# Shift and scale of the modulation summed along rows on VectorE, in a two-block transformer kernel on one core

## The chip, the core and the metric

The kernel runs on one core of a Trainium2 chip. The core has five engines that run side by side and wait for each other through semaphores: TensorE (matmuls, PE in the profile), VectorE (DVE), ScalarE (ACT), GpSimd (POOL) and SyncE (SP), which here issues most transfers. The metric is the device time of one execution in microseconds (us).

## What is computed

A batch of one sequence of 256 positions and 1024 features goes through two blocks. What the change touches is the adaptive modulation of the first block: a vector `c` of 1024 values is turned into nine rows of 1024, a shift, a scale and a gate for each of three sublayers.

```python
mods = (silu(c) @ w_ada + b_ada).reshape(1, 9, 1024)     # w_ada: 1024 x 9216, f32
shift = lambda i: mods[:, 3 * i]
scale = lambda i: mods[:, 3 * i + 1]
gate = lambda i: mods[:, 3 * i + 2][:, None, :]

n = rmsnorm(h, g_pre[0]) * (1 + scale(0)) + shift(0)      # sublayer 0: feed-forward
f = (silu(n @ w_gate) * (n @ w_up)) @ w_down
h = h + 0.5 * gate(0) * rmsnorm(f, g_post[0])
# sublayer 1: two attentions side by side ("mixer"); sublayer 2: a second feed-forward
# second block: two attention layers and two MLPs, no modulation
```

## The kernel before

All weights, 1024-column blocks of 128 partitions (512 KB each), come in one stream in the order of a list that `plan()` makes; `pump_one` issues transfers up to seven items ahead and works off one item. A weight item is split in two parts for precision: ScalarE casts it (`wh`, line 489) and VectorE takes the remainder (`wl`, line 495). Each product is then three matmuls: high by high, high by low, low by high. `nh` and `nl` are the same two parts of the normalised, modulated activations, with the features in the partitions and 256 positions along the row.

A modulation item is not used as a weight. `ada_item` handles it by VectorE: with the rows of `w_ada` in the partitions, a 128x1024 block is multiplied by one value of `silu(c)` per partition and added to a running tile `ada` (line 460; for the first block of a row a plain multiplication, line 458). After eight blocks (`k` from 0 to 7) `ada` holds partial sums that still have to be summed over the 128 partitions. For the shifts and scales of sublayers 1 and 2 (rows 3, 4, 6, 7) `ada_columns` does that by eight one-column matmuls with a vector of ones, which give the row as columns, features in the partitions: `ac_b` holds the shifts, `ac_a` the scales times the gain. For the gates (rows 2, 5, 8) `ada_gate` sums by matmuls with a matrix of ones. The gates' bias enters at the first block, through a tile `bz` that is zero but for its first row.

The shift and scale of sublayer 0 come in another cut, `ad0`, because the opening needs them piece by piece: an item `("ad0", k, q)` holds, for 128 features of the shift and 128 of the scale, four of the eight row blocks. ScalarE does the first of eight 128x256 multiplications (line 448), VectorE adds the other seven (line 450), and `reduce_` sums the tile over the partitions by two one-column matmuls.

`start_ffn` is the opening, written out by hand. `h[0]` and `h[1]`, the two halves of the positions, are squared and summed (line 607), scaled (`y`), transposed by TensorE (line 632) and kept as `yT`. Then the first seven column groups of the feed-forward (`M0`) are computed row block by row block: for each `k` from 0 to 7 `coefficients(k)` makes 128 features of `ac_b` and `ac_a`, applies them (`y2`, line 1023) and casts (line 1024), `low` makes `nl`, and `first(k, 0)` and `first(k, 1)` run 21 matmuls each against the items `s0` (gate and up weights, 448 KB each). I call one `k` a step. Each engine works its instructions in the order in which the code issues them.

Of the kernel before, what the change touches and what calls it, by code (L numbers as in the profile page):

```python
# [10 lines left out]
F32 = mybir.dt.float32  # L11
# [50 lines left out]
M0 = 7  # L62
# [45 lines left out]
def plan():  # L108
# [23 lines left out]
    for k in range(2):  # L132
        out += [(("ad0", k, 0), 1024), (("ad0", k, 1), 1024)]
        if k == 0:
            out.append((("s0", 0, 0), M0 * P))
    for k in range(8):
        out.append((("s0", k, 1), M0 * P))
        if k < 6:
            out += [(("ad0", k + 2, 0), 1024), (("ad0", k + 2, 1), 1024)]
        if k < 7:  # L140
            out.append((("s0", k + 1, 0), M0 * P))
# [54 lines left out]
def pack_stream(a):  # L196
# [11 lines left out]
    def piece(key):  # L208
        n = key[0]
        if n == "ad0":  # L210
            _, k, q = key
            w = a["w_ada"][0][512 * q:512 * q + 512]
            w = np.concatenate([w[:, P * k:P * k + P], w[:, D + P * k:D + P * k + P]], axis=1)
        elif n == "s0":
# [107 lines left out]
def model_kernel(ctx, tc, x, stream, cols, const, rows, bada, relb, onehot, out):  # L322
# [71 lines left out]
    for i in range(2):  # L394
        nc.sync.dma_start(h[1][:, 512 * i:512 * i + 512], x[tk(1), 512 * i:512 * i + 512])
# [16 lines left out]
    bz = cp.tile([P, D], F32, name="bz")  # L412
    pool.memset(bz, 0.0)
    nc.sync.dma_start(bz[0:1, :], bada[2:3, :])
# [15 lines left out]
    ada_end = {}  # L430
    bg = []

    def load(key, n, off):
        raw = w1k("raw0") if key[0] == "ad0" else rawp.tile([P, RAWC], F32, tag="raw", name="raw")
# [3 lines left out]
    def ada_item(key, raw):  # L438
        if key[0] == "ad0":
            _, k, q = key  # L440
            if q == 0:
                ada_acc["a"] = w256("ada")
            a = ada_acc["a"]
            for j in range(4):
                c = sc[:, 4 * q + j:4 * q + j + 1]
                r = raw[:, j * 2 * P:(j + 1) * 2 * P]
                if q == 0 and j == 0:
                    act.activation(a, r, AF.Copy, scale=c)
                else:
                    dve.scalar_tensor_tensor(a, r, c, a, op0=ALU.mult, op1=ALU.add)  # L450
            return
        _, j, k = key
        if k == 0:
            ada_acc[j] = w1k("ada")
        a = ada_acc[j]
        c = sc[:, k:k + 1]
        if k == 0 and j % 3 < 2:
            dve.tensor_scalar(a, raw, c, None, op0=ALU.mult)
        else:
            dve.scalar_tensor_tensor(a, raw, c, a if k else bz, op0=ALU.mult, op1=ALU.add)  # L460
        if k == 1 and j in (2, 5):
            nc.sync.dma_start(bz[0:1, :], bada[j + 3:j + 4, :])
        if k == 7:
            bg.append(ada_end[j](j, a))
            if j == 4:
                st["lo"] = "dve"
# [3 lines left out]
    def pump_one():  # L470
# [7 lines left out]
        if key[0] in ("ada", "ad0"):  # L478
# [25 lines left out]
    def pump(ahead=None):  # L504
        ahead = st["ahead"] if ahead is None else ahead
        while st["i"] < len(items):
            if items[st["i"]][0][0] not in ("ada", "ad0") and st["w"] >= st["rel"] + ahead + extra():
# [356 lines left out]
    bp1 = cp.tile([P, 72], F32, name="bp1")  # L864
    G = {}

    def ada_columns(j, a):
        for _ in range(4 if j == 3 else 2):
            yield
        ps = bank()  # L870
        for k in range(8):
            mm(ps[:, 2 * k:2 * k + 1], a[:, k * P:(k + 1) * P], ones[:, 0:1], start=(k == 0))
        v = ps.rearrange("p (k two) -> p k two", two=2)[:, 0:8, 0]
        i, sh = j // 3, j % 3 == 0
        if sh:
            dve.tensor_tensor(ac_b[:, i, :], v, cl[:, C_BADA + 8 * j:C_BADA + 8 * j + 8], op=ALU.add)
        else:
# [1093 lines left out]
```

## Time and profile before

| | |
|---|---|
| median of 3 runs | 1164.33 us (1160.9, 1164.33, 1165.6) |
| profiled execution | 1167.6 us |
| its span, first to last instruction | 1165.8 us |
| TensorE busy | 1120.3 us, 96% of the span |
| VectorE busy | 746.2 us, 64% |
| ScalarE busy | 603.4 us, 52% |
| transfers | 230.27 MB, mean 198 GB/s |

The shares are averages over stretches with different limits. What ends last in a stretch is read from the chain of work (what released each instruction, followed back from the end), from the timeline, and from the wait printed at a row's end in brackets with the instruction that ended it. The last part of the time, from 1165.8 to 1167.6 us, lies outside the span.

### The profile page before, as it was taken

Reading aid. Unit: us, or ns where it says so; the run is one execution under the profiler, and the core shown is the slowest. Engines: PE = TensorE matmul, PEld = TensorE weight load, DVE = VectorE, ACT = ScalarE, POOL = GpSimd, SP = SyncE. Lnnn points to the kernel's source line nnn. Section 1 sums busy time; section 2 is a strip of 40 time slices with the busy share of each in tenths; the row PEclk is TensorE's granted clock in tenths of the full one; section 3 lists DMA queues with packets and bytes.
Section 4 is the critical chain, followed back from the end, with each engine's and each line's share of the span. In section 5 each row is a group of like instructions: output and inputs, shape, how many; then the busy total and the mean of one; then the engine's idle time right before and its main releaser. Section 6 shows DMA issues by size and latency. Waiting matters only on the chain.

```text
span 1165.8 us, 18854 instructions
## 1 busy us (share of the span) xinstructions
PE 1120.3 (96%) x7268; PEld 1012.5 (87%) x7268; DVE 746.2 (64%) x1286; ACT 603.4 (52%) x1159; POOL 144.4 (12%) x152
## 2 busy tenths in 40 slices
PE   5999999899999899999999799999999999999997
PEld 5998999799888799999887678999998888999996
DVE  5987866689667776455656657555566746655554
ACT  5564444554576544343564566444457655544443
POOL 1001000204000300000058630000003200000001
PEclk9999999999999999999999999999999999999999
DMA  8978977468447385545544234655544523755540
GB/s 289 352 265 318 374 291 244 139 217 325 162 148 250 142 308 190 205 168 184 178 158 149 89 124 143 210 193 188 191 152 140 199 92 126 251 182 184 194 148 37
DMA packets 65920, 230.27 MB, mean 198 GB/s; under 512 B 7275, under 2 KB 8691, under 8 KB 65702
## 3 DMA queue, kind: packets, MB, share of 16 engines
q1 hardware_dynamic: 63798, 225.07, 55.8%
q10 hardware_dynamic: 1776, 3.29, 0.8%
q8 instruction: 57, 0.93, 0.3%
q0 software_dynamic: 256, 0.71, 0.2%
q14 instruction: 33, 0.27, 0.1%
HBM read 227.98 MB, written 2.63 MB: 198 GB/s over the span
## 4 chain that ended last, share of the span: by engine, by line
PE 76%; DVE 10%; ACT 7%; issue 3%; POOL 3%; DMA 0%; SPq 0%; POOLq 0%; ACTq 0%; DVEq 0%
PE mm L547 39%; PE acc L547 35%; DVE wl L495 2%; ACT wh L489 2%; POOL wl L495 2%; PE mm L632 1%; DVE ada L450 1%; DVE ada L460 1%; ACT junk L607 1%; ACT s L1491 1%; POOL sm L604 1%; ACT s L1346 1%; DVE s L1569 0%; DMA h<-in_x_dram 0%; DVE y L701 0%
## 5 line engine op out<-in xcount | busy, mean ns | idle before, releaser
L495 DVE TENSOR_TENSOR wl<-raw,wh 128x1024 fp32r<-128x1024 f32 (+4 forms) x318 | 380.4, 1210 | 86.5 <-ACT wh L489 86.4
L489 ACT ACTIVATE wh<-raw 128x1024 fp32r<-128x1024 f32 (+3 forms) x350 | 354.7, 1034 | 14.0 <-DMA raw<-in_stream_dram 12.9
L547 PE MATMUL mm<-nl,wh 128*128 128x256 f32 x1128 | 314.6, 284 | 0.0
L547 PE MATMUL mm<-nh,wh 128*128 128x256 f32 x1128 | 314.4, 284 | 0.0
L547 PE MATMUL mm<-nh,wl 128*128 128x256 f32 x1128 | 314.3, 283 | 0.0
L547 PEld LDWEIGHTS mm<-nl,wh 128*128 128x128 f32 x1128 | 214.5, 192 | 3.0
L547 PEld LDWEIGHTS mm<-nh,wh 128*128 128x128 f32 x1128 | 214.5, 192 | 3.0
L547 PEld LDWEIGHTS mm<-nh,wl 128*128 128x128 f32 x1128 | 214.2, 192 | 0.0
L547 PE MATMUL acc<-wl,fh 128*128 128x512 f32 x372 | 120.4, 390 | 1.5 <-DVE wl L495 1.5
L547 PE MATMUL acc<-wh,fh 128*128 128x512 f32 x372 | 120.9, 392 | 0.0
L547 PE MATMUL acc<-wh,fl 128*128 128x512 f32 x372 | 119.7, 389 | 0.0
L1089 ACT ACTIVATE rl<-mm 128x256 f32<-128x256 f32 x64 | 24.6, 384 | 160.9 <-PE mm L547 160.9
L495 POOL TENSOR_TENSOR wl<-raw,wh 128x512 fp32r<-128x512 f32 (+2 forms) x64 | 81.7, 1305 | 203.1 <-ACT wh L489 203.1
L604 POOL TENSOR_TENSOR sm<-sm,nhalf 128x1 f32<-128x1 f32 (+1 forms) x36 | 21.5, 597 | 631.4 <-DVE sm L613 566.9
L1090 DVE TENSOR_TENSOR ff<-rl 128x256 f32<-128x256 f32 x64 | 27.2, 425 | 102.5 <-ACT rl L1089 102.5
L914 ACT ACTIVATE sg<-mm 128x256 f32<-128x256 f32 x38 | 14.4, 382 | 137.8 <-PE mm L547 137.8
L547 PEld LDWEIGHTS acc<-wl,fh 128*128 128x128 f32 x372 | 69.9, 188 | 18.1 <-DVE wl L495 3.2
L547 PEld LDWEIGHTS acc<-wh,fl 128*128 128x128 f32 x372 | 69.9, 188 | 14.8
L547 PE MATMUL acc<-wh,nh 128*128 128x512 f32 (+3 forms) x208 | 79.2, 404 | 1.1 <-ACT nh L637 1.1
L547 PE MATMUL acc<-wh,nl 128*128 128x512 f32 (+3 forms) x208 | 75.3, 386 | 0.6 <-DVE nl L638 0.6
L547 PE MATMUL acc<-wl,nh 128*128 128x512 f32 (+3 forms) x208 | 75.1, 385 | 0.0
L547 PEld LDWEIGHTS acc<-wh,fh 128*128 128x128 f32 x372 | 65.5, 189 | 9.1
(322 smaller groups left out, 1638.3 us busy)
## 6 DMA issues: line engine op xcount, KB each, us to landing
raw<-in_stream_dram SPq DMA_DIRECT2D x395, 512.0 KB, 4.6
raw<-in_stream_dram SPq DMA_DIRECT2D x16, 448.0 KB, 6.5
raw<-in_stream_dram SPq DMA_DIRECT2D x8, 384.0 KB, 3.4
raw<-in_stream_dram SPq DMA_DIRECT2D x8, 292.0 KB, 3.2
gp<-in_rows_dram SPq DMA_DIRECT2D x3, 512.0 KB, 6.6
wide<-scr ACTq DMA_DIRECT2D x1, 1536.0 KB, 9.3
raw<-in_stream_dram SPq DMA_DIRECT2D x4, 320.0 KB, 3.0
h<-in_x_dram SPq DMA_DIRECT2D x4, 256.0 KB, 3.6
```

Source lines behind the costliest of these rows:

```text
L450: dve.scalar_tensor_tensor(a, r, c, a, op0=ALU.mult, op1=ALU.add)
L460: dve.scalar_tensor_tensor(a, raw, c, a if k else bz, op0=ALU.mult, op1=ALU.add)
L489: act.activation(wh[:, 0:n], raw, AF.Copy)
L495: e.tensor_tensor(wl[:, u:v], raw[:, u:v], wh[:, u:v].bitcast(F32), op=ALU.subtract)
L547: pe.matmul(o, l, r, start=start, stop=True, skip_group_check=True)
L604: pool.tensor_tensor(o, v, nhalf[:, 0:v.shape[-1]], op=ALU.pow)
L607: act.activation(junk(p_.shape[-1]), p_, AF.Square, scale=1.0 / math.sqrt(n) if scale is None else scale, accum_out=acc_)
L632: pe.transpose(tp[:, j * P:(j + 1) * P], src[:, j * P:(j + 1) * P], ident)
L914: act.activation(sg, ps[:, 0:S], AF.Silu)
L1089: act.activation(rl, ps[:, 0:S], AF.Relu)
L1090: dve.tensor_tensor(ff, rl, rl, op=ALU.mult)
L1346: act.activation(s[:, c], s[:, c], AF.Exp, bias=nm[:, t:t + 1], accum_out=rsum[:, 2 * t + j:2 * t + j + 1])
```

## The change

Shift and scale rows are packed transposed: 128 features in the partitions, all 1024 inputs along the row. One VectorE instruction multiplies such a block with `cb`, a tile that holds `silu(c)` in every partition, and sums along the row; the sum starts at the bias and lands in one column of `ac_b` (for a scale, times the gain, in `ac_a`). The sum over partitions on TensorE, `ada_columns`, `reduce_` and the cut `ad0` go. `cb` is made in the opening by eight TensorE matmuls, whose one side is a column of `c` read 128 times, and a silu on ScalarE. The gates keep their way, but their bias now starts the sum: eight ScalarE copies of 128x128 (the identity times a bias column) fill `ada` before the first block.

The opening is written in another order. The first modulation block is fetched ahead of `h[1]`, five more items behind it. The squares of `h[1]` are summed by VectorE with the same new operation. The transposes go by pairs of features' blocks into one bank each, the first step's activations are made straight from there, in both parts (`nh` and `y2`) by ScalarE from the same source, and the first group of matmuls runs high by high, high by low of the weights, then the low activations.

```diff
-        out += [(("ad0", k, 0), 1024), (("ad0", k, 1), 1024)]
+        out += [(("ada", 0, k), 1024), (("ada", 1, k), 1024)]
...
-            w = a["w_ada"][0][P * k:P * k + P, 1024 * j:1024 * j + 1024]
+            if j % 3 == 2:
+                w = a["w_ada"][0][P * k:P * k + P, 1024 * j:1024 * j + 1024]
+            else:
+                w = a["w_ada"][0][:, 1024 * j + P * k:1024 * j + P * k + P].T
...
+        i = j // 3
+        if j % 3 < 2:
+
+            dst, init, scale = (ac_b, cl[:, C_BADA + 8 * j + k:C_BADA + 8 * j + k + 1], 1.0) if j % 3 == 0 else \
+                (ac_a, bpg[:, 8 * i + k:8 * i + k + 1], cl[:, C_GPRE + 8 * i + k:C_GPRE + 8 * i + k + 1])
+            dve.tensor_tensor_reduce(out=raw, in0=raw, in1=cb, scale=scale, scalar=init, op0=ALU.mult, op1=ALU.add,
+                                     accum_out=dst[:, i, k:k + 1])
         else:
-            dve.scalar_tensor_tensor(a, raw, c, a if k else bz, op0=ALU.mult, op1=ALU.add)
...
+            if k == 0:
+                ada_acc[j] = w1k("ada")
+                for m in range(8):
+                    act.activation(ada_acc[j][:, m * P:(m + 1) * P], ident, AF.Copy,
+                                   scale=cl[:, C_BADA + 8 * j + m:C_BADA + 8 * j + m + 1])
+            a = ada_acc[j]
+            dve.scalar_tensor_tensor(a, raw, sc[:, k:k + 1], a, op0=ALU.mult, op1=ALU.add)
...
+        cps = [bank() for _ in range(2)]
+        for k in range(8):
+            mm(cps[k // 4][:, k % 4 * P:k % 4 * P + P], cl[:, C_C + k:C_C + k + 1].broadcast_to([P, P]), ident,
+               start=(k % 4 == 0))
+        raws.append(load(*items[0]))
+        for i in range(2):
+            nc.sync.dma_start(h[1][:, 512 * i:512 * i + 512], x[tk(1), 512 * i:512 * i + 512])
...
+        for i in range(2):
+            act.activation(cb[:, 512 * i:512 * i + 512], cps[i], AF.Silu)
+        r0 = inv_rms(ss[0])
...
+            dve.tensor_tensor_reduce(out=ys[1][hf], in0=half(1, hf), in1=half(1, hf), scale=1.0 / D, scalar=0.0,
+                                     op0=ALU.mult, op1=ALU.add, accum_out=ss[1][:, hf:hf + 1])
...
         def coefficients(k):
-            ps = red[0]
-            dve.tensor_tensor(ac_b[:, 0, k:k + 1], ps[:, 0:1], cl[:, C_BADA + k:C_BADA + k + 1], op=ALU.add)
...
+            src = yT[:, k, :] if k else tps[0][:, 0:S]
+            a, b = ac_a[:, 0, k:k + 1], ac_b[:, 0, k:k + 1]
+            act.activation(n[0][:, k, :], src, AF.Identity, scale=a, bias=b)
             y2 = w256("y2")
-            act.activation(y2, yT[:, k, :], AF.Identity, scale=ac_a[:, 0, k:k + 1], bias=ac_b[:, 0, k:k + 1])
-            act.activation(n[0][:, k, :], y2, AF.Copy)
+            act.activation(y2, src, AF.Identity, scale=a, bias=b)
```

VectorE in a step of the opening, before: partial sums with the two coefficient instructions between them, then `nl` of the next step and the remainders of two weight items.

```order
L450 SCALAR_TENSOR_TENSOR ada<-raw_225,sc,ada 128x256 x3
L1019 TENSOR_TENSOR ac_b<-mm,cl 128x1
L1020 SCALAR_TENSOR_TENSOR ac_a<-mm,bp_115,cl 128x1
L450 SCALAR_TENSOR_TENSOR ada<-raw_231,sc,ada 128x256 x4
L1028 TENSOR_TENSOR nl<-y_346,nh 128x256
L495 TENSOR_TENSOR wl<-raw,wh 128x896 x2
```

After, in the same step (`ISA` is the new operation and, below it, the read of its accumulator):

```order
L439 ISA raw_217,ac_b<-raw_217,cb,cl 128x1024
L439 ISA ac_b 128x1
L439 ISA raw_220,ac_a<-raw_220,cb,bpg,cl 128x1024
L439 ISA ac_a 128x1
L996 TENSOR_TENSOR nl<-y_315,nh 128x256
L481 TENSOR_TENSOR wl<-raw,wh 128x896 x2
```

Seven partial sums and two coefficient instructions have become two reductions with a read each; the coefficients of a step are made two steps ahead, and no TensorE work stands between them and ScalarE.

TensorE at the start of the program, before: the transposes of `y`, the sum of the first partial sums over the partitions, the first matmuls.

```order
L632 MATMUL mm<-kc,y 128x128 x16
L547 MATMUL mm<-onesr,ada 128x1 x2
L547 MATMUL acc<-nh,wh 128x256 x4
L547 MATMUL mm<-nh,wh 128x256 x3
L547 MATMUL acc<-nl,wh 128x256 x4
L547 MATMUL mm<-nl,wh 128x256 x3
```

After (`mm<-kc,cl` are the copies of `c` into all partitions):

```order
L533 MATMUL mm<-kc,cl 128x128 x8
L984 MATMUL mm<-kc,y 128x128 x16
L533 MATMUL acc<-nh,wh 128x256 x4
L533 MATMUL acc<-nh,wl 128x256 x4
L533 MATMUL acc<-nl,wh 128x256 x4
L533 MATMUL mm<-nh,wh 128x256 x3
```

The two matmuls on `ada` that stood ahead of the first step's matmuls are gone, eight on `cl` now stand ahead of the transposes, and in the first group the weights' low part comes ahead of the activations' low part.

ScalarE where the opening ends and the remainder of the feed-forward begins, before: the casts of two weights, then the silu of the seven column groups (`sg`), their cast (`Fh`) and the next weights.

```order
L489 ACTIVATE wh<-raw 128x1024 x2
L420 DMA kc<-in_const_dram 128x512
L914 ACTIVATE sg<-mm 128x256 x2
L918 ACTIVATE Fh<-sg 128x256
L489 ACTIVATE wh<-raw 128x1024
L914 ACTIVATE sg<-mm 128x256
L918 ACTIVATE Fh<-sg 128x256
```

After:

```order
L475 ACTIVATE wh<-raw 128x1024 x2
L415 DMA kc<-in_const_dram 128x512
L880 ACTIVATE sg<-mm 128x256
L445 ACTIVATE ada<-kc,cl 128x128 x8
L880 ACTIVATE sg<-mm 128x256
L884 ACTIVATE Fh<-sg 128x256
L475 ACTIVATE wh<-raw 128x1024
L880 ACTIVATE sg<-mm 128x256
```

Eight copies that start the first gate's sum now stand between the first two `sg`, ahead of the next weights' casts.

## Rows read from the trace of the kernel before

**Rows 1.** The page's part 4: the chain that ended last, shares by engine.

```profile
PE 76%; DVE 10%; ACT 7%; issue 3%; POOL 3%; DMA 0%; SPq 0%; POOLq 0%; ACTq 0%; DVEq 0%
```

**Rows 2.** Timeline, opening: start us, us, engine, line, operation, out<-in, count [idle before]

```profile
7.87 0.63 ACT L607 ACTIVATE junk<-h 128x512 bf16<-128x512 f32 x1 [1.04 <-DMA h<-in_x_dram]
...
8.92 0.56 POOL L604 TENSOR_TENSOR sm<-sm,nhalf 128x1 f32<-128x1 f32 x1 [1.90 <-DVE sm L613]
...
9.51 1.33 ACT L993 ACTIVATE y<-h,sm 128x512 f32<-128x512 f32 x2 [0.92 <-POOL sm L604]
...
16.50 0.60 ACT L1023 ACTIVATE y<-yT,ac_b,ac_a 128x256 f32<-128x256 f32 x1 [3.32 <-DVE ac_a L1020]
...
17.45 0.93 ACT L489 ACTIVATE wh<-raw 128x896 fp32r<-128x896 f32 x1
...
18.44 1.23 PE L547 MATMUL acc<-nh,wh 128*128 128x256 f32 x4 [2.36 <-ACT wh L489]
...
28.10 0.64 PE L547 MATMUL acc<-nh,wh 128*128 128x256 f32 x4
```

**Rows 3.** Windows: stretch, length, busy by engine, TensorE's granted clock, DMA share, GB/s

```profile
2.00:15.00 13.00, 3.94 (x16) 3.14 (x16) 4.98 (x12) 7.23 (x17) 3.18 (x6) 1.00 0.95 346
18.00:28.00 10.00, 9.56 (x46) 9.47 (x47) 9.20 (x21) 4.30 (x8) 0.00 (x0) 1.00 0.78 273
30.00:57.00 27.00, 26.44 (x216) 25.68 (x214) 26.11 (x57) 14.07 (x23) 0.00 (x0) 1.00 0.97 358
```

**Rows 4.** Timeline of one step of the opening, VectorE and TensorE

```profile
33.79 2.09 DVE L495 TENSOR_TENSOR wl<-raw,wh 128x896 fp32r<-128x896 f32 x2
...
35.80 1.52 DVE L450 SCALAR_TENSOR_TENSOR ada<-raw,sc,ada 128x256 f32<-128x256 f32 x3
...
36.18 0.50 PE L547 MATMUL mm<-onesr,ada 128*128 128x1 f32 x4
...
36.55 0.72 PE L547 MATMUL acc<-nh,wh 128*128 128x256 f32 x4
...
39.38 0.42 DVE L1028 TENSOR_TENSOR nl<-y,nh 128x256 fp32r<-128x256 f32 x1
...
39.49 0.74 PE L547 MATMUL acc<-nh,wh 128*128 128x256 f32 x4 [0.19 <-ACT wh L489]
...
39.71 2.08 DVE L495 TENSOR_TENSOR wl<-raw,wh 128x896 fp32r<-128x896 f32 x2
```

**Rows 5.** Chain of work in order of time: start us, us, what

```profile
67.68 11.88 PE mm L547 x99
```

**Rows 6.** VectorE's groups by form (busy us, mean ns); last row: tile ljk, min/median/max ns

```profile
L460 DVE SCALAR_TENSOR_TENSOR ada<-raw,sc,ada 128x1024 f32<-128x1024 f32 x49 | 62.8, 1283 | 0.0
...
L1488 DVE CUSTOM_DVE_ANT_0 s<-mm,cmaskw 128x256 f32<-128x256 f32 x24 | 10.1, 420 | 21.2 <-PE mm L547 21.2
...
L1488 DVE CUSTOM_DVE_ANT_0 s<-mm,cmaskw 128x128 f32<-128x128 f32 x24 | 6.8, 285 | 0.0
...
L1488 DVE DVE_READ_ACCUMULATOR2_ANT sm<- 128x1 f32 x48 | 3.9, 82 | 0.0
...
L1500 DVE CUSTOM_DVE_ANT_0 ljk<-lamin x2: 217/221/225, 573.9 to 574.2; 128x64 f32<-128x64 f32 x2
```

**Rows 7.** Timeline of TensorE, the first row of shifts behind the opening

```profile
159.83 1.84 PE L547 MATMUL mm<-onesr,ada 128*128 128x1 f32 x16
```

**Rows 8.** Chain of work in order of time, first mixer and its end

```profile
273.28 0.66 DVE ada L458
...
276.30 1.19 DVE ada L460
...
362.87 1.68 PE mm L547 x16
```

**Rows 9.** Timeline: VectorE behind the opening, ScalarE in the first mixer

```profile
70.46 1.22 DVE L495 TENSOR_TENSOR wl<-raw,wh 128x1024 fp32r<-128x1024 f32 x1
...
365.08 2.18 ACT L644 ACTIVATE db<-mm,cl 128x128 fp32r<-128x128 f32 x8 [2.50 <-PE mm L632]
```

More of the change, by code (lines that the diff above doesn't have):

```diff
@@ L138, in plan @@
         if k < 6:
[L139 removed]
+            out += [(("ada", 0, k + 2), 1024), (("ada", 1, k + 2), 1024)]
         if k < 7:
@@ L321, in model_kernel @@
 @with_exitstack
-def model_kernel(ctx, tc, x, stream, cols, const, rows, bada, relb, onehot, out):
+def model_kernel(ctx, tc, x, stream, cols, const, rows, relb, onehot, out):
     nc = tc.nc
@@ L438, in ada_item @@
     def ada_item(key, raw):
[L439 to L451, printed above, removed]
-        _, j, k = key
[L453 to L458, printed above, removed]
-        else:
-            dve.scalar_tensor_tensor(a, raw, c, a if k else bz, op0=ALU.mult, op1=ALU.add)
[L461 to L466, printed above, removed]
+        _, j, k = key
+        i = j // 3
[4 more added lines that the diff above has]
+                                     accum_out=dst[:, i, k:k + 1])
+        else:
+            if k == 0:
[5 more added lines that the diff above has]
+            dve.scalar_tensor_tensor(a, raw, sc[:, k:k + 1], a, op0=ALU.mult, op1=ALU.add)
+            if k == 7:
+                bg.append(ada_gate(j, a))
+        if k == 7 and j == 4:
+            st["lo"] = "dve"
     raws = []
@@ L506, in pump @@
         while st["i"] < len(items):
-            if items[st["i"]][0][0] not in ("ada", "ad0") and st["w"] >= st["rel"] + ahead + extra():
+            if items[st["i"]][0][0] != "ada" and st["w"] >= st["rel"] + ahead + extra():
                 if not spare or ahead < NR:
@@ L863, in model_kernel @@
     ac_b = cp.tile([P, 3, 8], F32, name="ac_b")
-    bp1 = cp.tile([P, 72], F32, name="bp1")
+    bpg = cp.tile([P, 24], F32, name="bpg")
     G = {}
[L867 to L877, printed above, removed]
-            tmp = small(8)
-            dve.tensor_tensor(tmp, v, bp1[:, 8 * j:8 * j + 8], op=ALU.add)
-            dve.tensor_tensor(ac_a[:, i, :], tmp, cl[:, C_GPRE + 8 * i:C_GPRE + 8 * i + 8], op=ALU.mult)
     def ada_gate(j, a):
@@ L981, in start_ffn @@
         yT = big(F32, "yT")
-        dve.tensor_scalar(bp1, cl[:, C_BADA:C_BADA + 72], 1.0, None, op0=ALU.add)
-        ss = [small(2) for _ in range(2)]
-        for t in range(2):
-            for hf in range(2):
-                square_sum(half(t, hf), D, ss[t][:, hf:hf + 1])
-        tps = []
-        for t in range(2):
-            r = inv_rms(ss[t])
-            ys = [w512("y") for _ in range(2)]
-            for hf in range(2):
-                if t:
-                    act.activation(ys[hf], half(t, hf), AF.Copy, scale=r)
-                else:
-                    dve.tensor_scalar(ys[hf], half(t, hf), r, None, op0=ALU.mult)
-            tps += [transposes(ys[hf], 4) for hf in range(2)]
+        dve.scalar_tensor_tensor(bpg.rearrange("p (a b) -> p a b", b=8),
+                                 cl[:, C_BADA:C_BADA + 72].rearrange("p (a b) -> p a b", b=24)[:, :, 8:16], 1.0,
+                                 cl[:, C_GPRE:C_GPRE + 24].rearrange("p (a b) -> p a b", b=8), op0=ALU.add, op1=ALU.mult)
@@ L997, in start_ffn @@
+        r1 = inv_rms(ss[1])
+        for hf in range(2):
+            act.activation(ys[1][hf], half(1, hf), AF.Copy, scale=r1)
         pump_one()
         pump_one()
-        for i, tp in enumerate(tps):
-            act.activation(yT[:, 4 * (i % 2):4 * (i % 2) + 4, tk(i // 2)], tp.rearrange("p (a b) -> p a b", a=4), AF.Copy)
-        acc = [abank() for _ in range(4)] + [bank() for _ in range(M0 - 4)]
-        sums = [ada_acc["a"]]
-        red = [None]
-        def ada_half():
-            pump_one()
-            if sums[-1] is not ada_acc["a"]:
-                sums.append(ada_acc["a"])
```

71 lines of the change are left out of this document (36 added, 35 removed).

## The prediction

> **What bounds the kernel now.** I read the chain of work that ended last first: TensorE holds 76% of it, VectorE 10%, ScalarE 7% [rows 1]. So the kernel is a TensorE kernel with a few stretches where something else ends last, and the worth of an edit depends on the stretch it lies in. The change lies in four stretches: the opening (the first 68 us), the rest of the first feed-forward, the first mixer, and the start of the second feed-forward.
>
> The opening next, in order of time. Its first real matmul starts at 18.44 [rows 2], long after the inputs have landed, because VectorE first walks through partial sums (eight quarter-tile instructions for row block 0), TensorE sums them over the partitions, VectorE adds the bias, ScalarE applies it and casts the weights. Then come eight steps of 42 matmuls. [...] From 33.79 to 39.71 the same VectorE instruction comes back after 5.92 us [rows 4], while 42 matmuls at 0.12 us need 5.04 us. What fills 5.92 us is VectorE, without a gap: two weight remainders 2.09, seven partial sums (three of them 1.52), the coefficients, the remainder of the activations 0.42. TensorE also carries four small matmul passes a step for the sum over the partitions (0.37 us from 36.18 to 36.55) and a wait of 0.19 us for ScalarE [rows 4]. The opening's last matmul is followed by the feed-forward's first at 67.7 [rows 5].
>
> **The change, part by part.** *What VectorE does in a step.* Seven quarter-tile instructions with ScalarE's one, and the two coefficient instructions, give way to two 128x1024 instructions that multiply and sum along the row, each with a read of the accumulator. That size of the new operation is not in the trace. Its small forms are: 420 ns for 256 columns, 285 ns for 128 [rows 6], so 1.05 ns a column and 285 + 896 x 1.05 = 1230 ns for 1024, plus up to 0.06 us for a scalar read from memory (an estimate from the two groups of 1024 columns with and without one, 1283 [rows 6] and 1.22 us [rows 9]). The read is 82 ns [rows 6]. An instruction of 1283 ns occupies the chain for 1.19 us [rows 8], since the next starts under its tail; I take 1.20 us each, 1.31 at most. A step is then 2 x 1.20 + 2.09 + about 0.35 = 4.8 us (at most 5.1) against TensorE's 5.04. VectorE stops being the bound, just.
>
> *TensorE in a step* loses the four small passes, and the coefficients no longer come out of PSUM, so ScalarE need not wait for them. Steps two to eight took from 28.10 to 67.7, 39.6 us; seven steps of 5.04 are 35.3. That is 4.3 us. The first step loses the passes alone: 42 x 0.215 = 9.0 instead of 9.66, 0.6 us.
>
> *The start.* Transfers: the first 512 KB weight block now stands ahead of the second half of x. That half landed at 7.87 [rows 2]; half a megabyte at 346 GB/s [rows 3] is 1.5 us, so 9.4. Behind it, in series: its sum of squares on VectorE, now by the new operation (128x512, 0.69 by the slope, and the read), the small add and GpSimd's power 0.56, two ScalarE scalings 1.33, the cast of the first weights 0.93, the modulation 0.60 [rows 2], and 0.5 for the small add and hand-offs: 9.4 + 0.8 + 0.56 + 1.33 + 0.93 + 0.6 + 0.5 = 14.1 us. The two new reductions for block 0 (2.4 us after 10.3, so 12.7) and the eight TensorE broadcasts with ScalarE's silu of them (an estimate: sixteen passes of 0.21 to 0.25 us from 3 on, then two instructions of 0.6, done before 9) lie beside that. First matmul 14.1 instead of 18.44: 4.3 us. If the landing is no later than before, 2 us more; if the queue interleaves the six early transfers, it may be 17, so the term lies between 1.4 and 6.
>
> *Transfers in a step* are two blocks of 512 KB and two of 448 KB, 1.97 MB. At 5.04 us that asks for 390 GB/s, and the stretch from 30 to 57 us moved 358 with the engines 97% busy [rows 3]. This is the next thing late: 0.45 us a step, some 2.5 us over the steps that still fetch blocks of modulation. Against it stands VectorE's lead of about one step over TensorE (it reduces block k+2 while TensorE runs block k). I charge 0.3 us, and keep 0 and 3. The opening: 4.3 + 0.6 + 4.3 - 0.3 = 8.9 us saved.
>
> *The four rows of shift and scale behind the opening.* Each was summed over the partitions by 16 TensorE passes, a burst that took 1.84 us to its last end at the first of them [rows 7] and 1.68 us of the chain of work at the last [rows 8]; they go. 4 x 1.7 = 6.8 us saved, 5 if what waits behind one of them was late anyway. Their 32 reductions stand where 32 accumulations stood; in the feed-forward VectorE has room for any difference.
>
> *In the first mixer* it has none: there VectorE's accumulations are in the chain, the first of a row at 0.66 us in a faster form, the others at 1.19 [rows 8]. The fast one becomes 1.20 (+0.5), some seven others cost 0.0 to 0.1 more: +0.7 us, between 0 and 1.5.
>
> *The gates' bias* was a zeroed tile with one row fetched into it; it becomes eight ScalarE copies of 128x128. Eight of about that size took 2.18 us [rows 9]. Three times: behind the opening, in the first mixer, in the second feed-forward. Behind the opening VectorE waits in order for them, and with it the weights of the next pair; these were ready at 70.46 + 1.22 = 71.7 [rows 9], TensorE asks for them 48 matmuls after 67.7, at 73.5. The cover is 1.8 us of 2.2: +0.4. In the mixer ScalarE feeds TensorE by turns: +0.7, between 0 and 2.2. In the second feed-forward the same cover as in the first holds: 0.
>
> Sum: 8.9 + 6.8 - 0.7 - 0.4 - 0.7 = 13.9 us saved. The profiled execution took 1167.6 us (span 1165.8), which gives 1153.7 (span 1151.9). Its time is 3.3 above the median of the three runs, 1164.33, so the time to expect is 1164.3 - 13.9 = 1150.4.
>
> [...] The one reduction in the trace whose two sources both lie in SBUF as f32 took 221 ns for 64 columns [rows 6]; the line through the other two forms gives 285 - 64 x 1.05 = 218. It ran at full rate. [...]
>
> **Rivals.** *The reductions run at half rate.* Then each one of 1024 columns costs 1.08 us more (another 1.05 ns a column): 2.2 us a step, 7.0 in all, VectorE stays the bound and the opening gains nothing; in the mixer eight of them add 8 us. 1164.3 - 6.8 + 8 + 1.8 = 1167. Against it stands the 221 ns.
>
> *The opening is fed too slowly.* The second half of x lands late enough for a first matmul at 17 instead of 14, or 358 GB/s is a ceiling and VectorE's lead is used up: the opening gains 3 to 6 instead of 8.9, and the time is 1153 to 1156. For it: the transfers are 97% busy already.
>
> *TensorE reaches its higher level sooner.* It now works from about 3 us on (the broadcasts, then the transposes), and with the first step at 0.12 us a matmul up to 4 us more are saved: 1146 to 1147, or less where the transfers stop it. Before, 16 transposes up to 12 us did not bring it about.
>
> *Slower: TensorE stays at its lower level.* The place is the opening: a first matmul at 14 runs with everything else barely ready, and if waits keep the level down, each matmul costs 0.095 us more than at 0.12. With all 294 after the first step that is 28 us: 1164.3 - 13.9 + 28 = 1178. It decides from about 150 such matmuls on, three and a half steps. Against it: before, the level rose in spite of a wait in every step, and was kept with one of 0.2 us in each.
>
> **How the numbers follow.** Forecast as worked out, 1146 to 1155: 0.62. Fed too slowly, 1153 to 1157: 0.18. Higher level sooner, 1143 to 1148: 0.10. Half rate, about 1167: 0.05. Lower level kept, up to 1178: 0.05. The likeliest gives 1150.4. The range runs from 1143.5 (nearly all of the fast case) to 1157 (all of the slowly fed one), which leaves out half rate, the lower level and the tails. Some 0.5% of this kernel's time, 5.8 us, is about what a measurement tells from no change: faster by more, below 1158.5, has the first three cases, 0.89 with a little taken off for their tails; within it lie half rate and those tails, 0.07; slower has the last, 0.04.
>
> **What would show it.** Right: the first 128x256 matmul near 14 us; VectorE's 128x1024 reductions at 1.2 to 1.3 us; from the second step on 5.0 to 5.1 us a step with VectorE waiting now and then; the feed-forward's first matmul near 58.8 (67.7 less 8.9); no small passes before the mixer; some eight ScalarE copies at three places. Wrong: a reduction of 2 us or more; matmuls at 0.21 us beyond the first step; VectorE waiting for a transfer in each step of the opening; TensorE idle by more than 1 us behind the opening, which would be the copies.

## The result, and the profile after

The changed kernel took 1145.93 us (median of four runs, 1145.35 to 1150.09) beside 1163.37 us for the kernel before on the same chip: a ratio of 0.9854, with an interval from 0.9831 to 0.9876; the medians are 17.4 us apart. The forecast was 1150.4, the range 1143.5 to 1157. A second series gave 1146.36 beside 1163.47 (0.9864, 0.9837 to 0.9891).

The profiled spans are 1165.8 and 1143.9 us, 21.9 apart, more than the medians; 4.4 us of that are told in the section on the event. In the page of the changed kernel (busy time, then the chain that ended last) VectorE has lost some work, and its share of the chain falls from 10% [rows 1] to 8%; the rest is TensorE as before:

```profile
PE 1102.8 (96%) x7188; PEld 994.8 (87%) x7188; DVE 741.0 (65%) x1276; ACT 607.3 (53%) x1173; POOL 146.7 (13%) x151
...
PE 75%; DVE 8%; ACT 7%; POOL 4%; issue 3%; DMA 2%; POOLq 0%; SPq 0%; ACTq 0%; DVEq 0%
```

The opening, from the timeline (start, length, engine, line, operation, count, and in brackets the idle time before and what ended it); it answers to [rows 2]:

```profile
3.10 3.78 PE L533 MATMUL mm<-kc,cl 128*128 128x128 f32 x16 [3.10 <-DMA kc<-in_const_dram]
...
7.14 0.55 POOL L590 TENSOR_TENSOR sm<-sm,nhalf 128x1 f32<-128x1 f32 x1 [6.04 <-DVE sm L599]
...
8.27 1.11 PE L984 MATMUL mm<-kc,y 128*128 128x128 f32 x8 [1.39 <-DVE y L971]
8.52 0.69 DVE L973 CUSTOM_DVE_ANT_0 y<-h 128x512 f32<-128x512 f32 x1
...
9.13 0.69 DVE L973 CUSTOM_DVE_ANT_0 y<-h 128x512 f32<-128x512 f32 x1
...
10.00 1.28 DVE L439 CUSTOM_DVE_ANT_0 raw<-raw,cb,cl 128x1024 f32<-128x1024 f32 x1
10.16 1.52 POOL L590 TENSOR_TENSOR sm<-sm,nhalf 128x1 f32<-128x1 f32 x1 [2.47 <-DVE sm L599]
...
11.72 1.34 ACT L977 ACTIVATE y<-h,sm 128x512 f32<-128x512 f32 x2 [4.00 <-POOL sm L590]
...
12.49 1.97 PE L984 MATMUL mm<-kc,y 128*128 128x128 f32 x8 [3.11 <-ACT y L977]
...
12.96 0.93 ACT L475 ACTIVATE wh<-raw 128x896 fp32r<-128x896 f32 x1
...
14.40 1.22 PE L533 MATMUL acc<-nh,wh 128*128 128x256 f32 x4
...
17.12 0.59 PE L533 MATMUL mm<-nh,wh 128*128 128x256 f32 x3
...
21.29 0.75 PE L533 MATMUL acc<-nh,wh 128*128 128x256 f32 x4 [0.34 <-ACT wh L475]
```

The first matmul of the steps starts at 14.40 instead of 18.44. Ahead of it stand the two reductions of row block 1's squares (8.52 and 9.13), GpSimd's power (10.16, for 1.52 us), ScalarE's scaling, the cast of the weights and the modulation, in the order that the prediction gave. TensorE's broadcasts (3.10) start at 0.24 us a pass; the first eight transposes (8.27) run at 0.14 us each, the next eight (12.49) at 0.25. The matmuls run at 0.21 us until about 17 (eight from 15.42 to 17.12) and at 0.12 after it: this upper level comes 2.7 us after the first matmul; before, it came 8.7 us after it, from 18.44 [rows 2] to 27.10 (timeline of before):

```profile
27.10 0.81 PE L547 MATMUL acc<-nh,wl 128*128 128x256 f32 x4
```

So the first step took 6.9 us (14.40 to 21.29), with a wait of 0.34 us for ScalarE at its end.

The windows that answer to [rows 3]: busy time by engine, TensorE's granted clock, share of the DMA engines, GB/s:

```profile
2.00:15.00 13.00, 7.41 (x35) 6.50 (x36) 6.26 (x15) 6.36 (x15) 4.14 (x6) 0.82 1.01 362
18.00:28.00 10.00, 9.66 (x81) 9.46 (x80) 9.45 (x14) 5.05 (x8) 0.00 (x0) 1.00 1.01 401
30.00:57.00 27.00, 26.09 (x218) 25.89 (x217) 23.97 (x33) 15.29 (x20) 0.00 (x0) 1.00 1.02 396
```

From 18 us on the transfers moved 396 to 401 GB/s, with the DMA engines' share at 1.01 to 1.02; from 30 to 57 us they had moved 358 at a share of 0.97 [rows 3]. What waited for whom between 14 and 60 us (total, times, longest), and the new reductions' times (min/median/max in ns):

```profile
ACT wh L475 <- DMA raw<-in_stream_dram: 12.5, 10, 1.8
...
PE acc L533 <- ACT wh L475: 1.2, 2, 0.9
```

```profile
L439 DVE CUSTOM_DVE_ANT_0 raw<-raw,cb,cl x24: 1276/1280/3415, 10.0 to 292.9; 128x1024 f32<-128x1024 f32 x24
...
L439 DVE CUSTOM_DVE_ANT_0 raw<-raw,cb,bpg x24: 1339/1342/1346, 11.2 to 334.5; 128x1024 f32<-128x1024 f32 x24
```

ScalarE's cast of the weights waits for a transfer ten times, TensorE for the cast twice. VectorE's step is now 4.86 us without a gap, from 37.48 to 42.34 (5.92 before [rows 4]), beside 5.04 for TensorE's 42 matmuls:

```profile
37.48 2.14 DVE L481 TENSOR_TENSOR wl<-raw,wh 128x896 fp32r<-128x896 f32 x2
...
39.53 1.28 DVE L439 CUSTOM_DVE_ANT_0 raw<-raw,cb,cl 128x1024 f32<-128x1024 f32 x1
...
40.74 1.34 DVE L439 CUSTOM_DVE_ANT_0 raw<-raw,cb,bpg 128x1024 f32<-128x1024 f32 x1
...
41.26 2.06 ACT L475 ACTIVATE wh<-raw 128x896 fp32r<-128x896 f32 x2 [1.79 <-DMA raw<-in_stream_dram]
...
42.34 2.10 DVE L481 TENSOR_TENSOR wl<-raw,wh 128x896 fp32r<-128x896 f32 x2
```

A reduction takes 1280 ns with one scalar read from memory, 1342 with two, and the next VectorE instruction starts 1.20 to 1.27 us later. One of the 48 took 3.4 us: it started at 104.03, while a GpSimd instruction ran from 103.24 to 106.37. ScalarE's swiglu that follows the opening's last matmul starts at 57.8 instead of 67.8.

The table gives how much sooner a point of the program was reached than in the profile of before, in us: the end of the opening (first swiglu), the first feed-forward's gate (first use of the new bias), the end of the first feed-forward (first use of its gate, behind the place where rows 3 and 4 were summed before), the mixer's last softmax, the second feed-forward's gate (behind rows 6 and 7), and the first step of the MLP, behind the differential attention, which the change doesn't touch. "Again" is the second series of the changed kernel; the other columns are experiments described below.

| point | before at | changed | again | opening only | rows only | bias fetched | VectorE extra | both cures | before, factor by ScalarE |
|---|---|---|---|---|---|---|---|---|---|
| end of the opening | 67.8 | 10.0 | 12.1 | 7.4 | 0.4 | 11.9 | 4.1 | 10.3 | 0.4 |
| gate, first feed-forward | 121.0 | 9.5 | 11.6 | 6.9 | -0.1 | 11.9 | 3.6 | 10.3 | 0.4 |
| end of first feed-forward | 209.2 | 12.0 | 14.0 | 7.0 | 2.4 | 14.4 | 6.0 | 12.8 | 0.5 |
| last softmax of the mixer | 307.5 | 11.6 | 12.9 | 5.8 | 1.3 | 15.0 | 4.9 | 11.0 | 0.5 |
| gate, second feed-forward | 450.5 | 17.7 | 17.6 | 7.9 | 6.1 | 21.1 | 11.0 | 17.0 | 2.3 |
| MLP's first step | 714.9 | 22.2 | 22.1 | 12.4 | 4.5 | 21.0 | 14.0 | 17.0 | 2.2 |

### The profile page after: what moved, and what is told of

It is laid out like the page before. It is cut to its first block, busy times and chain, and to the rows that moved or that the text cites. A ratio compares the mean times of both kernels' runs of the same rounds, so it can differ in the third digit from the quotient of the medians.

```text
span 1143.9 us, 18675 instructions
## 1 busy us (share of the span) xinstructions
PE 1102.8 (96%) x7188; PEld 994.8 (87%) x7188; DVE 741.0 (65%) x1276; ACT 607.3 (53%) x1173; POOL 146.7 (13%) x151
## 4 chain that ended last, share of the span: by engine, by line
PE 75%; DVE 8%; ACT 7%; POOL 4%; issue 3%; DMA 2%; POOLq 0%; SPq 0%; ACTq 0%; DVEq 0%
PE mm L533 37%; PE acc L533 37%; POOL wl L481 2%; DVE wl L481 2%; ACT wh L475 2%; DMA raw<-in_stream_dram 1%; PE mm L618 1%; ACT junk L593 1%; DVE raw L439 1%; POOL sm L590 1%; ACT s L1466 1%; ACT s L1321 1%; ACT ada L445 1%; DVE s L1544 0%; DVE y L687 0%
## 5 line engine op out<-in xcount | busy, mean ns | idle before, releaser
L533 PEld LDWEIGHTS acc<-wh,fl 128*128 128x128 f32 x372 | 69.9, 188 | 14.6
## 6 DMA issues: line engine op xcount, KB each, us to landing
wide<-scr ACTq DMA_DIRECT2D x1, 1536.0 KB, 10.3
```

The lines of the kernel that those rows point to most:

```text
L533: pe.matmul(o, l, r, start=start, stop=True, skip_group_check=True)
```

## Experiments

### The two halves of the change

Opening only: the changed kernel, with rows 3, 4, 6 and 7 accumulated and summed over the partitions as before.

```diff
-        if j % 3 < 2:
+        if j < 2:
...
+        elif j % 3 < 2:
...
+                dve.scalar_tensor_tensor(ada_acc[j], raw, sc[:, k:k + 1], ada_acc[j], op0=ALU.mult, op1=ALU.add)
+            if k == 7:
+                bg.append(ada_columns(j, ada_acc[j]))
```

> The changed kernel, with rows 3, 4, 6 and 7 of the modulation computed as before (accumulated over eight blocks, then summed over the partitions by 16 small TensorE passes each); the new opening and the copies of the gates' bias stay. Theory: the changed kernel's gain of 17.4 us is made of about 10 in the opening (the feed-forward's first matmul came 10.05 us sooner by the two traces), less about 0.5 for the copies, and of about 8 from the four rows. Then this kernel is 9 to 10 us faster than before, about 1154. Rival one, the rows are worth what was forecast of them, 5.3 with the mixer's cost: 12 us faster here, about 1151.5. Rival two, nearly all of it is the opening: 15 or more faster, below 1149.

Rows only: the kernel before with these four rows by reductions and the gates' bias by copies.

```diff
+        nc.gpsimd.dma_start(cb, rows[:, 4352:5376].broadcast_to([P, D]))
...
+        if j % 3 < 2:
+            dve.tensor_tensor_reduce(out=raw, in0=raw, in1=cb, scale=scale, scalar=init, op0=ALU.mult, op1=ALU.add,
+                                     accum_out=dst[:, i, k:k + 1])
...
+            for m in range(8):
+                act.activation(a[:, m * P:(m + 1) * P], ident, AF.Copy,
+                               scale=cl[:, C_BADA + 8 * j + m:C_BADA + 8 * j + m + 1])
```

> The kernel before, its opening untouched, with rows 3, 4, 6 and 7 by one reduction for each 128 features (the vector c is fetched spread over the partitions after the opening) and the gates' bias by ScalarE copies. Theory: 7 to 8.5 us faster than before, about 1156, so that this one and the opening alone add up to the whole gain. Rival one: 4.5 to 6 faster, as forecast, about 1158.5. Rival two, nearly all of the gain lies in the opening: at most 2 faster.

Measured: the opening alone 1156.79 us beside 1162.76, ratio 0.9954 (0.9935 to 0.9972), some 5 us; the rows alone 1163.35, ratio 0.9992 (0.9974 to 1.001), nothing that can be told. Together 6, not 17, so no theory held by the medians: the rows alone fit their second rival's "at most 2 faster", but its reason, that nearly all of the gain lies in the opening, fails by the opening alone. Three things in the traces bear on it. First, the opening-only run had a late transfer that the two traces of the changed kernel don't have (timeline):

```profile
22.53 0.95 ACT L483 ACTIVATE wh<-raw 128x896 fp32r<-128x896 f32 x1 [3.07 <-DMA raw<-in_stream_dram]
...
23.53 0.82 PE L541 MATMUL acc<-nh,wh 128*128 128x256 f32 x4 [2.36 <-ACT wh L483]
...
24.80 1.05 PE L541 MATMUL acc<-nl,wh 128*128 128x256 f32 x4
```

TensorE waited 2.36 us, its passes were slow again behind the wait (the next of four take 0.82 to 1.05 us, where 0.64 is usual at the upper level), and the opening ended 2.6 us later than in the changed kernel. Second, the rows-only run has the 5.2 us event of the next part, the opening-only one hasn't; the former's twelve times have three from 1156.6 to 1159.1 and nine from 1162.1 to 1165.1, the latter's go from 1153.7 to 1162.1. Third, the copies of the gates' bias are paid in both. By the table, ahead of the event's place, the halves are 7.9 and 6.1 us sooner. To that come the 2.6 us of the late transfer and the copies' 0.5 to 1.5, paid twice (0.5 is measured behind the opening, the rest is an estimate for the mixer). Off it go 1.5 to 2.1 us by which the profile of before was itself late behind the mixer (see *Rows 6 and 7* below), counted twice in the halves. That is 15.0 to 16.6, where the whole is 17.7. So the split is told by the traces, to some 3 us, and not by the medians.

The rows-only kernel fetched `c` from 9.1 us on, in the opening and not after it; its opening ended at 67.4, as in the others with the old opening (67.1 to 67.8).

### An event in the differential attention

In some traces one VectorE instruction of two columns takes 5.2 us. From the timeline of before, and below it the same place in the changed kernel:

```profile
634.13 5.24 DVE L1566 SCALAR_TENSOR_TENSOR sm<-sm,nlam 128x2 f32<-128x2 f32 x1
...
634.35 1.28 POOL L1481 TENSOR_TENSOR ro<-t,t 128x512 f32<-128x512 f32 x1
...
635.58 2.56 POOL L495 TENSOR_TENSOR wl<-raw,wh 128x512 fp32r<-128x512 f32 x2
...
638.07 1.28 POOL L1481 TENSOR_TENSOR ro<-t,t 128x512 f32<-128x512 f32 x1
```

```profile
616.35 0.27 DVE L1541 SCALAR_TENSOR_TENSOR sm<-sm,nlam 128x2 f32<-128x2 f32 x1
...
616.56 1.26 POOL L1456 TENSOR_TENSOR ro<-t,t 128x512 f32<-128x512 f32 x1
616.65 2.77 DVE L1544 SCALAR_TENSOR_TENSOR s<-s,sm 128x256 f32<-128x256 f32 x2
```

In both VectorE's factor starts 0.2 us ahead of GpSimd's `ro`. In one it is done in 0.27 us, in the other it ends only when GpSimd's four instructions in a row are done (634.35 to 639.35). The stretch from the second feed-forward's end to the MLP took 134.7 to 136.4 us in the five traces with it (before, rows only, bias fetched, TensorE filled, x first) and 130.3 to 131.8 in the five without it (changed, again, opening only, VectorE extra, before with broadcasts). So it comes with either opening, and 4.4 of the 21.9 us between the two profiled spans are this, not the change. Times beside the other engine are longer elsewhere too: GpSimd's power took 1.52 us beside a reduction and 0.55 without one, a reduction 3.4 beside GpSimd and 1.28 in the median. Here VectorE's factor, recorded as starting first, ended at 639.37, 0.02 us after the last of GpSimd's four instructions. So GpSimd is the likely cause, not a shown one; what lets the factor pass in one run and not in another stays open.

The changed kernel was run again, and two pairs make this place alike in both kernels. In the first pair VectorE alone makes the weight remainders of that attention; in the second ScalarE makes the factor, and the changed kernel also has the fetched bias of the part below.

```diff
-LOS = {("dqk", 1, 0): "pool", ("woa", 6): "dve", ("wdkv", 0): "pool"}
+LOS = {("dqk", 1, 0): "dve", ("woa", 6): "dve", ("wdkv", 0): "pool"}
```

```diff
-            dve.scalar_tensor_tensor(cf, su[:, 0:2], nlam, inv[:, 2:4], op0=ALU.mult, op1=ALU.mult)
+            for t in range(2):
+                act.activation(cf[:, t:t + 1], sl[:, t:t + 1], AF.Copy, scale=inv[:, 2 + t:3 + t])
```

> The changed kernel once more, for its spread beside the kernel before. In the trace of before, and of the rows-only kernel, one VectorE instruction of two columns in the differential attention took 5.2 us, behind GpSimd's instructions; in the traces of the changed kernel and of the opening-only one it took 0.27. Theory: which of the two happens is chance, so this kernel's times fall into groups some 4 to 5 us apart, about 1145.5 and 1150. Rival: the changed kernel always gets the short one, and its times stay within 2 us of 1145.5.

> The kernel before, with VectorE alone making the weight remainders of the differential attention (GpSimd made them there). Beside the next kernel it tells what the change is worth without the 5.2 us event. Theory: no VectorE instruction is held up by more than 1.5 us, the times spread less, and the two kernels differ by 14 to 16 us instead of 17.4. Rival: the event has no part in the difference, and it stays at 17 to 18.

> The changed kernel with the same edit as the kernel before it in this list: VectorE alone makes the weight remainders of the differential attention. Theory: 14 to 16 us below that kernel. Rival: 17 to 18 below it.

> The kernel before, with the two-column factor of the differential attention made by ScalarE (three small instructions a head) instead of the VectorE instruction that took 5.2 us in some traces. Theory: the event goes with that instruction; the stretch between the second feed-forward and the first MLP takes the shorter of its two lengths (130.3 us by the traces without the event, 134.7 to 136.4 with it), and the median comes down to the lower end of before, 1160 to 1162. Rival: the wait passes to the next VectorE instruction behind it, and the time stays at 1163 or rises.

> The changed kernel with the same factor by ScalarE and, as in the kernel with the fetched bias, without the copies of the gates' bias. Theory: 1141 to 1143.5, some 3 to 5 faster than the changed kernel; and 17 to 20 below the kernel ahead of it in this list, of which about 1.5 are the copies: then the event has at most a small share in the change's 17. Rival: 13 to 16 below it: the event's luck was some 3 us of the change's gain. If the wait only passes on, about 1147.

Measured: the changed kernel again 1145.8 to 1147.8 four times and 1152.0 once, which agrees with the theory, though that slower run has no trace. First pair 1166.01 and 1153.96 (ratios to before 1.0017, from 1.0002 to 1.0032, and 0.9918, from 0.9896 to 0.994), 12.1 us apart (forecast for it 14 to 16, so less than either theory); no instruction of that line is above 1.3 us, but both kernels are slower, since the stretch takes 135.2 and 135.8 us. Second pair 1166.1 and 1150.0 (1.0021, from 1.001 to 1.0032, and 0.9882, from 0.9863 to 0.9901), 16.1 apart, at the edge of the lower of its two forecasts (13 to 16, and 17 to 20). The rival for the kernel before held, for the wait passes on: ScalarE's factor stands behind a cast, and the next two VectorE instructions run beside GpSimd and take 2.58 us, where the same two took 0.75 in the kernel before, from 639.41 on with GpSimd done (timeline of the kernel before with ScalarE's factor):

```profile
634.12 0.28 ACT L1566 ACTIVATE sm<-sm,nlam 128x2 f32<-128x2 f32 x1
...
634.63 2.74 POOL L495 TENSOR_TENSOR wl<-raw,wh 128x512 fp32r<-128x512 f32 x2
...
634.94 2.58 DVE L1572 SCALAR_TENSOR_TENSOR s<-s,sm 128x256 f32<-128x256 f32 x2 [1.47 <-ACT sm L1569]
```

The stretch takes 134.8 us in both, and the changed kernel of this pair is 3 us above the 1147 expected for a wait that passes on. So neither pair is a cure, and no version here beats the changed kernel by its median. But where both kernels pass this place alike, the change is worth 12.1 us, or 16.1 with the fetched bias, which by the estimate above is 0.5 to 1.5 of it. How often the event falls into each kernel's timed runs can't be read from times, so the share that it has in the 17.4 stays open between about 1 and 5 us.

### The copies of the gates' bias

```diff
-                for m in range(8):
-                    act.activation(ada_acc[j][:, m * P:(m + 1) * P], ident, AF.Copy,
-                                   scale=cl[:, C_BADA + 8 * j + m:C_BADA + 8 * j + m + 1])
...
+        if key[0] == "ada" and key[1] % 3 == 2 and key[2] == 0:
+            ada_acc[key[1]] = w1k("ada")
+            pool.memset(ada_acc[key[1]], 0.0)
+            nc.gpsimd.dma_start(ada_acc[key[1]][0:1, :], bada[key[1]:key[1] + 1, :])
```

> The changed kernel without the 24 ScalarE copies of the gates' bias: the accumulator is zeroed by GpSimd and gets one fetched row when the first block's load is issued. Theory: the copies cost what the trace shows behind the opening (10.05 sooner before them, 9.5 after) and about as much in the mixer: 0.5 to 1.5 us faster than the changed kernel, 1144.5 to 1145.5. Rival: they lie beside other work and nothing changes, within 0.3 us. Other side: GpSimd's zeroing disturbs VectorE, and it is slower by 0.5 or more.

Measured: 1148.41 us, ratio to before 0.9878 (0.9858 to 0.9897), 2 above the changed kernel's second series, where 0.5 to 1.5 less was expected. Its trace is 3.5 us ahead of the changed kernel's at the second gate (21.1 and 17.6 to 17.7), has the event behind it, and is 1.1 to 1.2 late after that; whether GpSimd's zeroing costs anything isn't settled. The line of the copies in the changed kernel:

```profile
L445 ACT ACTIVATE ada<-kc,cl x24: 387/390/413, 58.1 to 380.1; 128x128 f32<-128x128 f32 x24
...
  DVE ada L448: 4.1, 3
```

Between the end of the opening and the first gate the changed kernel loses 0.5 us (10.0 to 9.5; the same 0.5 in "again", in opening only and in VectorE extra), the two kernels without copies lose none (11.9 and 11.9; 10.3 and 10.3). In the mixer the losses with copies (0.4 to 1.2) and without (a gain of 0.6, a loss of 1.8) overlap, so their cost there is not settled. From the mixer's last softmax to the second gate 4.7 to 6.1 are gained with them, 6.0 and 6.1 without: they cost nothing that can be seen there, 1.4 at most.

### What bounds the new steps

VectorE extra: one more 128x1024 reduction in each of the six steps that have a pair, into scratch.

```diff
+            if j == 1 and k >= 2:
+                dve.tensor_tensor_reduce(out=raw, in0=raw, in1=cb, scale=1.0, scalar=0.0, op0=ALU.mult, op1=ALU.add,
+                                         accum_out=small(1))
```

> The changed kernel with one more 128x1024 reduction on VectorE in each of the six steps of the opening that have a pair (its result goes to scratch). Theory: the steps got shorter because VectorE was relieved, to just under TensorE's 5.04 us; with 1.28 us more VectorE has 6.1 us a step and is the bound again: 5 to 6.5 us slower than the changed kernel, about 1151.5, and steps of 6.0 to 6.2 us. Rival: transfers are what limits the steps, VectorE has room, and it costs 0 to 2 us.

Measured: 1156.95 us; the opening ends 5.9 later than in the changed kernel, VectorE's step is 6.08 us (from 35.89 to 41.97), and now TensorE and ScalarE wait for VectorE:

```profile
ACT nh L993 <- DVE ac_a L439: 7.4, 5, 2.7
...
PE acc L536 <- DVE nl L999: 3.1, 5, 0.6
```

The theory held for the steps: VectorE has 0.18 us of room in a step of the changed kernel (4.86 beside 5.04) and not more. The extra reduction, with no scalar from memory, took 1.22 us, so each such scalar costs 0.06. The median is 10.6 above the second series (5 to 6.5 forecast), the trace's end 8.2 later; what comes on behind the opening is not explained.

TensorE filled: 22 transposes into an unused bank, where TensorE waited from 9.4 to 12.5.

```diff
+            if t:
+                fill = abank()
+                for k in range(22):
+                    pe.transpose(fill[:, k % 4 * P:k % 4 * P + P], ys[0][0][:, k % 4 * P:k % 4 * P + P], ident)
```

> The changed kernel with 22 transposes of row block 0 into an unused PSUM bank, placed between the transposes of the two row blocks, where TensorE waits from 9.4 to 12.5 us. Theory: with TensorE at work through the gap the level is still the upper one at the first step; the second block's eight transposes take 1.1 us instead of 1.97 and the first 42 matmuls about 5.1 instead of 6.9, and since the weights of the following step land no sooner (TensorE already waited 0.34 us for them) the opening ends at most 0.7 us sooner, within the measurement. Rival: the level is not set by the work just before, and the first matmuls still take 0.21 us; or the weights are not the limit, and the opening ends 1.5 to 2 us sooner.

Measured: 1148.28 us (ratio to before 0.9869, 0.9844 to 0.9895), no gain. TensorE's timeline:

```profile
9.81 3.38 PE L986 MATMUL acc<-kc,y 128*128 128x128 f32 x22
13.03 1.04 PE L988 MATMUL mm<-kc,y 128*128 128x128 f32 x8
14.29 0.74 PE L533 MATMUL acc<-nh,wh 128*128 128x256 f32 x4 [0.22 <-ACT nh L994]
...
15.54 0.64 PE L533 MATMUL acc<-nl,wh 128*128 128x256 f32 x4
...
21.70 0.74 PE L533 MATMUL acc<-nh,wh 128*128 128x256 f32 x4 [1.61 <-ACT wh L475]
```

The level stayed up: the block's transposes took 1.04 us, and four matmuls 0.64 to 0.74 instead of 1.05 to 1.22 from the start. But the next step's weights were not there: TensorE waited 1.61 us, started the second step at 21.70 (21.29 in the changed kernel), and the opening ended at 57.8, as without the filling. So here and in the changed kernel the landing of the second step's weights sets the start of the seven steps, not the level; from there it is TensorE's 5.04 us a step and some 1 us of waits. In three other traces (again, bias fetched, both cures) TensorE waits for no weights, but those of the second step were cast only 0.05 to 0.7 us before it started, and a sooner level could give no more than that.

Before with broadcasts: the kernel before, with the eight early broadcasts, unused.

```diff
+        for k in range(8):
+            mm(cps[k // 4][:, k % 4 * P:k % 4 * P + P], cl[:, C_C + k:C_C + k + 1].broadcast_to([P, P]), ident,
+               start=(k % 4 == 0))
```

> The kernel before with the eight early TensorE broadcasts of the changed kernel added, their result unused. Theory: the level at which the first step runs comes from what TensorE does just ahead of it; here it waits between 12.3 and 15.1 and between 16 and 18.4 as before, so the first step still takes 9.2 to 9.7 us and the opening ends at 67 to 68. Rival: the early work brings the upper level, the first step takes 7 or less, and the opening ends 1 to 3 us sooner, unless VectorE holds it up.

Measured: one run, 1162.41, and a first step of 9.2 us (17.66 to 26.86), the number expected, but the theory behind it fell. TensorE's timeline:

```profile
3.05 3.79 PE L547 MATMUL mm<-kc,cl 128*128 128x128 f32 x16 [3.05 <-DMA kc<-in_const_dram]
...
14.31 0.98 PE L547 MATMUL mm<-onesr,ada 128*128 128x1 f32 x4 [3.55 <-DVE ada L450]
17.66 1.23 PE L547 MATMUL acc<-nh,wh 128*128 128x256 f32 x4 [2.36 <-ACT wh L489]
...
20.71 0.64 PE L547 MATMUL acc<-nh,wl 128*128 128x256 f32 x4
...
22.31 0.61 PE L547 MATMUL mm<-onesr,ada 128*128 128x1 f32 x4 [0.61 <-DVE ada L450]
...
26.86 0.74 PE L547 MATMUL acc<-nh,wh 128*128 128x256 f32 x4 [1.33 <-ACT wh L489]
```

The upper level came 3 us after the first matmul (four passes in 0.64 at 20.71) instead of 8.7, though TensorE still waits 3.5 and 2.4 us in between. In all nine traces with the broadcasts, the filled one left out, it came 2.2 to 4.4 us after the first matmul. Without them it came about 9 us after it in three of four; in the fourth, rows only, it came after 4.0 (TensorE's timeline):

```profile
17.96 1.22 PE L557 MATMUL acc<-nh,wh 128*128 128x256 f32 x4 [2.36 <-ACT wh L499]
...
21.93 0.52 PE L557 MATMUL mm<-nh,wl 128*128 128x256 f32 x3
...
27.15 0.74 PE L557 MATMUL acc<-nh,wh 128*128 128x256 f32 x4 [1.33 <-ACT wh L499]
```

So the early broadcasts go with the sooner level, but it also comes without them; that they bring it is likely and not shown. What was gained here went into waits: 0.61 us for VectorE's partial sums (22.31) and 1.33 for ScalarE's cast (26.86). Rows only has the same 1.33 and a first step of the same 9.2. The opening ended at 67.1; the five traces with the old opening have 67.1 to 67.8.

x first: the second row block ahead of the first block of modulation in the queue.

```diff
-        raws.append(load(*items[0]))
         for i in range(2):
             nc.sync.dma_start(h[1][:, 512 * i:512 * i + 512], x[tk(1), 512 * i:512 * i + 512])
+        raws.append(load(*items[0]))
```

> The changed kernel with the second block of x fetched ahead of the first block of modulation, as before the change. Theory: that block of x is there 1 to 1.5 us sooner, the first matmul starts near 13.3 instead of 14.4, and the opening ends where it did (55.7 to 60.4 in five traces with the new opening), since the steps wait for transfers and their sum is the same. Rival: the order counts, and the opening ends 1 us or more sooner, below 55; or the first reduction, now later, holds up the first matmul, above 15.

Measured: one run, 1150.90, with the event. The first matmul started at 14.11, not 13.3: VectorE's scaling of block 0 (from 7.44) was followed at 8.24, without a wait, by its squares of block 1; the opening ended at 57.1, within the range expected. One run with the event can't show what this order is worth in time; the opening shows no gain.

## Why the prediction was right

The time and its sign were right, and the sum is near what can be rebuilt from the traces; some of its terms are off and cancel, which is luck.

*Opening.* Forecast 8.9 sooner; 7.4 to 12.1 in the six traces with the new opening as it is, 10.1 in the mean (9.6 beside the mean of the five old openings). The first matmul (forecast 14.1) came at 14.40, in the others at 13.44 to 15.51, by when x landed (the first block's last squares at 4.98 to 6.47, VectorE's wait for the second block 0 to 1.33). In the changed kernel two misses cancel there: VectorE squared the second half of x from 8.52 on without a wait, where the forecast had it land at 9.4, and GpSimd's power took 1.52 us, not 0.56. The first step, forecast 9.0, took 6.9 (6.8 to 8.7 in the six): what failed is the prediction's sentence against the rival of the higher level, that 16 transposes had not brought it about before; with the broadcasts it came sooner in every trace (4.4 us after the first matmul or less), and once without them (4.0). The sum's 0.215 us for a matmul of the first step stands in no row as such; 46 passes in 9.56 us [rows 3] are 0.21, as in the changed kernel until 17. Its 0.12 is 99 in 11.88 us [rows 5], as in the changed kernel after that. Steps two to eight, forecast 35.3 and 0.3 for transfers, took 36.5 in the changed kernel and 36.9 in opening only, but 35.3 to 35.4 in the other four: the charge was too small where a transfer came late, and 358 GB/s was no ceiling, for they reached 396 to 410. So two of the rivals came true in part, the sooner level and, in some runs, the slow feeding, and the second takes back what more of the first would give: TensorE filled ended the opening no sooner.

*The reductions* took 1.28 and 1.34 us for a forecast of 1.23 to 1.29, pitch 1.20 to 1.27 for 1.20. The rival of half rate, with 1.08 us more for each, is refuted for this instruction with two f32 sources in SBUF. VectorE's step was 4.86 us, forecast 4.8.

*Rows 3 and 4* saved 2.4 to 2.5 us by the end of the first feed-forward in every trace with the new rows, rows only among them (-0.1 to 2.4): the lower end (5 for four rows), not 3.4. *Rows 6 and 7*: from the mixer's last softmax to the second gate the new rows are 4.7 to 6.1 sooner than before, but kernels with the old rows are 1.5 to 2.1 sooner there too (0.5 to 2.3 in the last column, 5.8 to 7.9 in opening only, 0.7 to 2.2 in before with broadcasts), so before's own profile was slow there; 2.6 to 4.6 are left, forecast 3.4. *Mixer:* 0.4 to 1.2 lost, forecast 1.4. *Copies:* 0.5 behind the opening (0.4), nothing in the second feed-forward (0).

With the middle of each: 10 + 2.5 + 3.6 - 0.8 - 0.5 = 14.8 us, forecast 13.9; the pairs that pass the differential attention alike give 12.1 and 14.6 to 15.6. The timed 17.4 is more, and the event in a stretch that no step of the prediction looked at is the likely rest, not a shown one.

## What to carry to other kernels

Relieving the bound engine brings the next limit into view, and with it its scatter: the old opening ended within 0.7 us in five traces, under VectorE, the new one within 4.7 in six, by when the transfers landed. Before adding up the halves of a change by their medians, compare the traces point by point, and look for instructions far above their group's median in stretches that the change doesn't touch. A term worth 2 us off another bound (the sooner level) is worth nothing until that bound is gone: with TensorE filled the opening ended at 57.8, as without.

## What the hardware showed beyond that

GpSimd's power on one column took 0.55 us with VectorE idle and 1.52 while VectorE's reduction with two SBUF sources ran (10.00 to 11.28; 1.52 to 1.53 in every trace with the new opening); that is 1 us on the way to the first matmul. A VectorE instruction of two columns took 5.24 us and ended with the last of four GpSimd instructions beside it; in another run, with the same lead to 0.01 us, it took 0.27. When the upper level comes in the first step varies: with eight broadcasts at 3 to 7 us it came 2.2 to 4.4 us after the first matmul, although TensorE waited 3.5 and 2.4 us in between in one of these runs; without them it came about 9 us after it in three runs and 4.0 in one. A VectorE reduction of 1024 columns takes 1.22 us, and 0.06 more for each scalar read from memory.
